# A float32 decoder trunk on one core: weights split in pairs of units, block sums over both depth halves, and one seven-product set computed plainly

## The chip, the cores and the metric

The kernel runs on one core of a Trainium2 chip. Times are device microseconds of that core. TensorE (PE in the profile) multiplies, VectorE (DVE) and ScalarE (ACT) do elementwise work, GpSimd (POOL) does small arithmetic and issues the DMAs that add into their destination, SyncE (SP) issues the other DMAs. Weights are read from memory once, as they are used.

## What is computed

A trunk of four layers on 256 rows of width 1024. Each layer is a half-step SwiGLU FFN, a token mixer with memory attention, and another half-step FFN, each between two normalizations. The kinds of mixer follow one another as A, B, C, A.

```python
def swiglu_ffn(x, w_gate_up, w_down):
    gate, up = jnp.split(x @ w_gate_up, 2, axis=-1)
    return (jax.nn.silu(gate) * up) @ w_down

for i in range(DEPTH):
    kind, j = i % 3, i // 3
    g = norm_g[i]
    x = x + 0.5 * rms_norm(swiglu_ffn(rms_norm(x, g[0]), ffn_w_gate_up[i, 0], ffn_w_down[i, 0]), g[1])
    h = rms_norm(x, g[2])
    mem_n = rms_norm(mem, mem_norm_g[i])
    ...
    x = x + rms_norm(y, g[3])
    x = x + 0.5 * rms_norm(swiglu_ffn(rms_norm(x, g[4]), ffn_w_gate_up[i, 1], ffn_w_down[i, 1]), g[5])
```

All of it is in float32. The hidden width of an FFN is 2816, that is 22 tiles of 128.

## The kernel before

**Three matmuls for one.** Every operand is split into a high part and a rest, `hi` and `lo`, of a type that PE multiplies in one pass. A product is then three matmuls: hi by hi, hi by lo, lo by hi. `split` (L311) makes both parts: ACT copies the source into `hi` (L312), and DVE subtracts `hi` from the source into `lo` (L313). Weights and activations go through it alike.

**The weight stream.** `plan()` lists all weight units in the order in which they are used. A unit has up to 1024 columns on 128 partitions, 512 KB. `load_next` (L244) fetches a raw unit into one of RAW = 5 buffers, on SP's queue. `split_next` (L291) takes the next unit of the plan, splits it into one `hi` and one `lo` tile of a ring of RING = 10, and fetches another raw unit. `take` hands a split unit to the code that multiplies; `slot(free)` is called after the matmuls of a unit, counts `free` units as released, and calls `pump`, which splits up to two units ahead while fewer than `released + RING - 1` have been split.

**An FFN** (`ffn`, L537) computes its hidden columns in six sets, `WIDTH = (4, 4, 2, 4, 4, 4)` tiles of 128. Set 0 runs while the second half of the rows is still being normalized: eight units, gate and up, are held for two passes (`first_set`). Sets 2 ("e") and 4 are plain: each unit is multiplied by both row halves, 12 matmuls of 512 columns a unit, and a set of four tiles has eight units. Sets 1, 3 and 5 are in `SEVEN`: gate and up for both row halves are a 2 x 2 block product, which `seven` (L635) makes with seven products instead of eight (Strassen's way, in Winograd's form). A product has two "S" units, one for each half of its depth (`h`), and each has six matmuls. The activations' block sums are made once an FFN (`sums`, L601).

**The weights' blocks.** For a seven-product set the four blocks b11, b12, b21, b22 of the weights are loaded raw into `quad` tiles (`load_quad`, L260), in eight loads of 512 KB, one a slot, in the order b11, b21, b12, b22. The operands of the seven products are b11, b21, b11 + (b12 + b22), b12 + b22, the third less b22, b21 plus the third, and b22. `operand` (L282) makes them half by half: when a half of b22 has been issued, a DMA of POOL's adds it into b12 (`gather`, L271); for operand 2 DVE adds b12 into b11 (L285) and another gather adds that into b21; for operand 4 DVE subtracts b22 from b11 (L288). An operand can be split only once all its loads have been issued (`can_split`, `quads_for`).

**The rest of an FFN.** In `seven`, products accumulate in three tiles of PSUM; intermediate sums are copied out by ACT (`snap`, L632) and combined by DVE (L644, L655, L661, L666, L667). `turned` transposes a finished set for the down projection and splits it into `hh` and `hl` (`eh` and `el` for set 2). `fill(n)` multiplies `n` units of the down projection ("D") between products; FILL says how many go where. The last eight D units are held for the two row halves; in the second pass the normalization of the first half (`ln_stages`, L361) and its transposes (L403) run beside it. The result of that is the next stage's `xt`.

**Mixers** take their weights from the same stream ("R", "C", "K", "V", "O" units). `snap` is a tag of four buffers, used for the copies above, for the squares of the normalization, for `xf` (the transposed activations that `sums` starts from) and for the memory's rows.

**The order on each engine** is made when the program is built: a planner goes through the instructions with its own estimates of their cost, and gives each engine the earliest instruction in program order that it holds ready. On the chip each engine then runs its list in that order, and what waits holds up what is behind it.

Of the kernel before, what the change touches and what calls it, by code (L numbers as in the profile page):

```python
# [10 lines left out]
F32 = mybir.dt.float32  # L11
F32R = mybir.dt.float32r
# [3 lines left out]
ALU = mybir.AluOpType  # L16
AX = mybir.AxisListType

P = 128
# [11 lines left out]
LN_EPS = 1e-5  # L31
BIG = 1e30
RING = 10
RAW = 5
HELD = 8
GRP = 4

# [18 lines left out]
WIDTH = (4, 4, 2, 4, 4, 4)  # L56
SETS = len(WIDTH)
FIRST = tuple(sum(WIDTH[:s]) for s in range(SETS))
SEVEN = (1, 3, 5)
FILL = {1: (2, 2), 2: (2,), 3: (2, 0), 4: (1, 1), 5: (2, 2)}  # L60
QUADS = 8


def ffn_chunks(l, f):
    order = []
    nd = 0

    def fill(n):
        nonlocal nd, order
        order += [("D", l, f, nd + i) for i in range(n)]  # L70
        nd += n

    for s in range(SETS):
        if s in SEVEN:
# [50 lines left out]
def load_order():  # L125
    order = []
    for key in plan():
        if key[0] != "S":
            order.append(key)
        elif key[4:] == (0, 0):  # L130
            order += quads(*key[1:4])
    return order


def unit_shape(key):
# [70 lines left out]
class Trunk:  # L206
    def __init__(self, ctx, tc, io):
        self.ctx, self.tc, self.nc, self.io = ctx, tc, tc.nc, io
        pool = lambda name, bufs=1, **kw: ctx.enter_context(tc.tile_pool(name=name, bufs=bufs, **kw))
        self.const = pool("const")  # L210
        self.wp = pool("wp")
        self.main = pool("main")
        self.small = pool("small", 4)
        self.ps = pool("ps", space=bass.MemoryType.PSUM)
        self.dram = pool("dram", space=bass.MemoryType.DRAM)
        self.plan = plan()
        self.offs = {}
# [5 lines left out]
        self.raw_order = [key for key in self.plan if key[0] != "S"]  # L223
        self.loaded = self.split_n = self.taken = self.released = 0
# [19 lines left out]
    def load_next(self):  # L244
        if self.loaded == len(self.raw_order):
            return
        key = self.raw_order[self.loaded]
        a, b = unit_shape(key)
        t = self.wp.tile([P, 1024], F32, tag="raw", name="raw", bufs=RAW)
        self.fetch(t[:, :a * b], key)  # L250
        self.raws.append((t, a * b))
        self.loaded += 1

    def new_quad(self, fp, l, f, s):
# [5 lines left out]
    def load_quad(self):  # L260
        key = self.quad_loads.popleft()
        q, h = key[4:]
        if h == 0:
            pool, tag = ((self.main, "mgh"), (self.quad_pool, "q22"), (self.main, "mgl"), (self.main, "rows"))[q]
            self.quad[q] = pool.tile([P, 2, 1024], F32, tag=tag, name="quad")
        self.fetch(self.quad[q][:, h, :], key)
        if q == 3:
            self.gather(self.quad[1][:, h, :], self.quad[3][:, h, :])

    def gather(self, x, y):  # L270
# [2 lines left out]
    def quads_for(self, key):  # L273
        if self.quad is None or self.quad_set != key[1:4]:
            return None
        return max(0, len(self.quad_loads) - (QUADS - ((2 * key[4] if key[4] < 2 else 6) + key[5] + 1)))

    def can_split(self):
        key = self.plan[self.split_n]
        return key[0] != "S" or self.quads_for(key) == 0  # L280

    def operand(self, op, h):  # L282
        b11, b12, b21, b22 = (t if t is None else t[:, h, :] for t in self.quad)
        if op == 2:
            self.nc.vector.tensor_tensor(out=b11, in0=b11, in1=b12, op=ALU.add)  # L285
            self.gather(b21, b11)
        elif op == 4:
            self.nc.vector.tensor_tensor(out=b11, in0=b11, in1=b22, op=ALU.subtract)  # L288
        return (b11, b21, b11, b12, b11, b21, b22)[op]

    def split_next(self):  # L291
        key = self.plan[self.split_n]
        hi = self.wp.tile([P, 1024], F32R, tag="hi", name="hi", bufs=RING)
        lo = self.wp.tile([P, 1024], F32R, tag="lo", name="lo", bufs=RING)
        if key[0] == "S":
            for _ in range(self.quads_for(key)):
                self.load_quad()
            self.split(hi, lo, self.operand(*key[4:]))
        else:
            t, n = self.raws.popleft()  # L300
            self.split(hi[:, :n], lo[:, :n], t[:, :n])
            self.load_next()
        self.ready.append((hi, lo))
        self.split_n += 1

    def pump(self, lag=1, most=2):
        while most and self.split_n < len(self.plan) and self.split_n < self.released + RING - lag and self.can_split():
            self.split_next()
            most -= 1

# [226 lines left out]
    def ffn(self, l, f, post_next, pre_next, last=False):  # L537
        nc, tc = self.nc, self.tc
        with tc.tile_pool(name=f"ffn{l}{f}", bufs=1, reuse_waits="tile") as fp:
# [15 lines left out]

            def turn_set(s, t):
                if t == 0:
                    if WIDTH[s] == 2:
                        hs[s] = tuple(fp.tile([P, 2, SEQ], F32R, tag=n, name=n) for n in ("eh", "el"))
                    else:  # L560
                        hs[s] = tuple(fp.tile([P, 4, SEQ], F32R, tag=n, name=n, bufs=2) for n in ("hh", "hl"))
                n = WIDTH[s]
                ps = self.rot()
                for k in range(n):
                    nc.tensor.transpose(ps[:, k * P:(k + 1) * P], T[s][t][:, k * P:(k + 1) * P], self.ident)  # L565
                self.split(*(h[:, :n, t * P:(t + 1) * P] for h in hs[s]),
                           ps[:, :n * P].rearrange("p (k t) -> p k t", k=n))
# [101 lines left out]
                product(s, 6, c, False, c12)  # L669
                fill(FILL[s][1])  # L670

            self.new_quad(fp, l, f, 1)
            first_set()
            left = sums()
            gn = {"pre": None}
# [102 lines left out]

    def mem_kv(self, l):
        nc = self.nc  # L780
        km = self.mp.tile([P, 2, SEQ], F32, name="km")
        vm = self.mp.tile([P, 2, SEQ], F32, name="vm")
        ps = self.rot().rearrange("p (a b) -> p a b", a=2)
        for c in range(2):
            self.cols_unit(ps[:, c, :], self.memg, self.take("K", l, c))
# [55 lines left out]
        return got[0]  # L841

    def q_mem(self, l, c0, xt):
        qm = self.mp.tile([P, 2, SEQ], F32, name="qm")
        ps = self.in_cols(l, c0, xt)
        self.nc.scalar.activation(out=qm, in_=ps, func=AF.Copy, scale=-0.125)
        return qm
# [500 lines left out]
```

## Time and profile before

| | us |
|---|---|
| median of 3 runs (lowest, highest) | 1889.15 (1886.43, 1889.77) |
| profiled execution | 1888.2 |
| its span, first to last instruction | 1886.4 |
| granted clock of TensorE, mean of the span | 0.996 |

| engine | busy, share of the span |
|---|---|
| TensorE, weight loads | 81% |
| VectorE | 81% |
| ScalarE | 60% |
| GpSimd | 8% |

Busy time of an engine is the time in which one of its instructions ran, by the profile. TensorE's matmuls overlap one another, so a busy TensorE need not be at its peak. A wait is the idle time of an engine just before an instruction, put down to what released it. The rows that carry the argument stand in the prediction.

### The profile page before, as it was taken

The page shows a single profiled execution, that of the slowest core. Times are in us where ns is not written, and L with a number is a line of the kernel's source. Part 1 is how long each engine was busy: PE and PEld are TensorE (multiplying, and loading weights), DVE is VectorE, ACT ScalarE, POOL GpSimd, SP SyncE. Part 2 cuts the span into 40 slices and gives each one's busy share as a digit, 9 for nine tenths or more (in the row PEclk, how much of TensorE's full clock was granted, in tenths as well). Part 3 has the DMA queues.
Part 4 walks back from the last instruction along what each step waited for, and adds up shares of the span by engine and source line. Part 5 has one row for each costly group of instructions (what it writes and reads, how often), then busy time and mean ns, then how long its engine had stood idle before and what let it go on. Part 6 is the DMA issues. An engine that isn't in the chain of part 4 may idle for free.

```text
span 1886.4 us, 25346 instructions
## 1 busy us (share of the span) xinstructions
PE 1842.0 (98%) x9310; PEld 1535.2 (81%) x9310; DVE 1537.1 (81%) x1868; ACT 1132.7 (60%) x1541; POOL 150.2 (8%) x211
## 2 busy tenths in 40 slices
PE   7999999999999999999999999999999999999998
PEld 5788887878788797778878889877788888987886
DVE  6888878987988768888789876879887988879884
ACT  5666656656665655656666666556665666656652
POOL 0000201000100100100010000010001000201000
PEclk9999999999999999999999999999999999999999
DMA  8886748776786662677668667358775786738862
GB/s 295 257 265 225 224 136 264 227 243 223 226 261 194 235 220 101 201 242 247 215 210 263 211 218 257 105 190 256 247 245 169 245 264 204 247 125 273 256 192 78
DMA packets 117692, 413.01 MB, mean 219 GB/s; under 512 B 13620, under 2 KB 18112, under 8 KB 117440
## 3 DMA queue, kind: packets, MB, share of 16 engines
q1 hardware_dynamic: 103568, 359.47, 54.2%
q0 software_dynamic: 14000, 51.92, 13.8%
q8 instruction: 73, 1.20, 0.3%
q14 instruction: 51, 0.42, 0.1%
HBM read 359.95 MB, written 1.06 MB: 191 GB/s over the span
## 4 chain that ended last, share of the span: by engine, by line
PE 41%; DVE 7%; DMA 3%; issue 2%; ACT 1%; POOL 1%; DVEq 0%; ACTq 0%; POOLq 0%
PE acc L696 12%; PE rot L624 9%; PE rot L337 5%; PE rot L339 5%; PE rot L338 5%; DVE lo L313 5%; PE acc L960 2%; DMA quad<-quad 2%; DMA quad<-in_w 1%; PE rot L565 1%; PE acc L880 1%; DVE quad L288 1%; PE rot L894 1%; PE rot L862 1%; ACT hi L312 0%
## 5 line engine op out<-in xcount | busy, mean ns | idle before, releaser
L313 DVE TENSOR_TENSOR lo<-raw,hi 128x1024 fp32r<-128x1024 f32 (+2 forms) x451 | 536.3, 1217 | 77.6 <-ACT hi L312 74.7
L312 ACT ACTIVATE hi<-raw 128x1024 fp32r<-128x1024 f32 (+2 forms) x451 | 463.2, 1051 | 198.3 <-DMA raw<-in_w 96.7
L312 ACT ACTIVATE hi<-quad 128x1024 fp32r<-128x1024 f32 x336 | 343.6, 1053 | 227.5 <-DVE quad L285 131.8
L313 DVE TENSOR_TENSOR lo<-quad,hi 128x1024 fp32r<-128x1024 f32 x336 | 397.5, 1219 | 20.7 <-ACT hi L312 19.9
L339 PE MATMUL rot<-hi,xtl 128*128 128x512 f32 (+3 forms) x816 | 312.8, 384 | 3.9 <-DVE xtl L313 3.9
L337 PE MATMUL rot<-hi,xth 128*128 128x512 f32 (+3 forms) x816 | 315.0, 386 | 0.4 <-ACT hi L312 0.4
L338 PE MATMUL rot<-lo,xth 128*128 128x512 f32 (+3 forms) x816 | 312.0, 382 | 0.3 <-DVE lo L313 0.3
L624 PE MATMUL rot<-hi,sums 128*128 128x512 f32 x768 | 255.1, 398 | 16.2 <-ACT snap L632 8.0
L696 PE MATMUL acc<-hi,hh 128*128 128x512 f32 x640 | 199.4, 391 | 0.0
L696 PE MATMUL acc<-lo,hh 128*128 128x512 f32 x640 | 198.9, 390 | 0.0
L696 PE MATMUL acc<-hi,hl 128*128 128x512 f32 x640 | 197.9, 390 | 0.0
L624 PEld LDWEIGHTS rot<-hi,sums 128*128 128x128 f32 x768 | 145.8, 190 | 52.9 <-ACT snap L632 12.3
L339 PEld LDWEIGHTS rot<-hi,xtl 128*128 128x128 f32 x816 | 153.7, 188 | 37.0 <-DVE xtl L313 8.3
L337 PEld LDWEIGHTS rot<-hi,xth 128*128 128x128 f32 x816 | 153.8, 189 | 29.2 <-ACT hi L312 1.0
L338 PEld LDWEIGHTS rot<-lo,xth 128*128 128x128 f32 x816 | 153.8, 188 | 29.2 <-DVE lo L313 0.5
L624 PE MATMUL rot<-lo,sums 128*128 128x512 f32 x384 | 151.2, 394 | 2.1 <-DVE lo L313 2.1
L271 POOL DMA_DIRECT2D quad<-quad x96 | 83.7, 897 | 837.6 <-DMA quad<-in_w 394.5
L696 PEld LDWEIGHTS acc<-hi,hl 128*128 128x128 f32 x640 | 119.6, 188 | 26.9 <-DVE hl L313 2.2
L696 PEld LDWEIGHTS acc<-lo,hh 128*128 128x128 f32 x640 | 119.9, 188 | 24.7
L696 PEld LDWEIGHTS acc<-hi,hh 128*128 128x128 f32 x640 | 119.7, 188 | 24.5
L624 PE MATMUL rot<-hi,xtl 128*128 128x512 f32 x288 | 112.1, 389 | 0.0
L624 PE MATMUL rot<-hi,xth 128*128 128x512 f32 x288 | 112.0, 389 | 0.0
(214 smaller groups left out, 2571.3 us busy)
## 6 DMA issues: line engine op xcount, KB each, us to landing
raw<-in_w SPq DMA_DIRECT2D x440, 512.0 KB, 4.8
quad<-in_w SPq DMA_DIRECT2D x192, 512.0 KB, 5.1
quad<-quad POOLq DMA_DIRECT2D x96, 512.0 KB, 4.7
gpre<-in_norm_g SPq DMA_DIRECT2D x8, 512.0 KB, 6.3
gpost<-in_norm_g SPq DMA_DIRECT2D x8, 512.0 KB, 3.4
memraw<-in_mem_t SPq DMA_DIRECT2D x32, 128.0 KB, 3.6
g<-in_norm_g SPq DMA_DIRECT2D x8, 512.0 KB, 6.7
raw<-in_w SPq DMA_DIRECT2D x8, 384.0 KB, 4.1
```

The costliest lines, as they stand in the source:

```text
L271: self.nc.gpsimd.dma_start(out=x, in_=y, accum_op=ALU.add)
L288: self.nc.vector.tensor_tensor(out=b11, in0=b11, in1=b22, op=ALU.subtract)
L312: self.nc.scalar.activation(out=hi, in_=src, func=AF.Copy)
L313: self.nc.vector.tensor_tensor(out=lo, in0=src, in1=hi.bitcast(F32), op=ALU.subtract)
L337: mm(out, a[0], b[0], start=start, stop=False)
L338: mm(out, a[0], b[1], start=False, stop=False)
L339: mm(out, a[1], b[0], start=False, stop=stop)
L565: nc.tensor.transpose(ps[:, k * P:(k + 1) * P], T[s][t][:, k * P:(k + 1) * P], self.ident)
L624: nc.tensor.matmul(ps, a[i], w[j][:, kk, :], start=fresh and h == kk == i == j == 0, stop=h == kk == i == 1, skip_group_check=True)
L696: mm(ys[t][:, n * 512:(n + 1) * 512], x, y[:, 0, n * 512:(n + 1) * 512], start=(j == 0 and x is a[0] and y is w[0]), stop=(j == NF - 1 and ...
L862: nc.tensor.transpose(ps[:, i * P:(i + 1) * P], blocks[b0 + i], self.ident)
L960: self.nc.tensor.matmul(o["y"][t][:, h * 512:(h + 1) * 512], x, y[:, 0, h * 512:(h + 1) * 512], start=(j == 0 and x is a[0] and y is w[0]) ...
```

## The change

- The ring holds pairs. `groups` joins neighbouring units of the plan that have the same kind and layer (for "S" units the two halves of one product). A pair is loaded by two DMAs into one raw tile of 2048 columns (RAW = 3 of them instead of 5 of 1024) and split by one ACT and one DVE instruction of 2048 columns, into one of five `hi` and five `lo` tiles. Where a pair's units are narrower than 1024, each is split by itself. `pump` counts units, and may split two groups a slot.
- Block sums go over both halves at once: one DVE instruction of 2048 columns for operands 2 and 4, and one gather of 1 MB into b21. All eight quads must have been issued ahead of operand 2.
- In set 1 b22 is added into b12 by DVE, not by a gather. Sets 3 and 5 keep the gathers, half by half.
- In the first FFN of layer 0 set 1 is plain: gate and up units, `fill(2)` after each.
- FILL of set 4 is (2, 0) instead of (1, 1), in all FFNs.
- Set 2 uses the two `hh` and `hl` buffers instead of its own `eh` and `el`; `km`, `vm` and `qm` of the mixers move from the mixer's pool to the `snap` tag.

```diff
-RAW = 5
+RAW = 3
...
-SEVEN = (1, 3, 5)
-FILL = {1: (2, 2), 2: (2,), 3: (2, 0), 4: (1, 1), 5: (2, 2)}
+FILL = {1: (2, 2), 2: (2,), 3: (2, 0), 4: (2, 0), 5: (2, 2)}
...
+def seven_sets(l, f):
+    return (1, 3, 5) if l or f else (3, 5)
...
+def groups(order):
+    out = []
+    for key in order:
+        last = out[-1] if out else []
+        if len(last) == 1 and last[0][:2] == key[:2] and (key[0] != "S" or last[0][:5] == key[:5]):
+            last.append(key)
+        else:
+            out.append([key])
+    return out
...
-        key = self.raw_order[self.loaded]
-        a, b = unit_shape(key)
-        t = self.wp.tile([P, 1024], F32, tag="raw", name="raw", bufs=RAW)
-        self.fetch(t[:, :a * b], key)
-        self.raws.append((t, a * b))
+        t = self.wp.tile([P, 2048], F32, tag="raw", name="raw", bufs=RAW)
+        for i, key in enumerate(self.raw_order[self.loaded]):
+            a, b = unit_shape(key)
+            self.fetch(t[:, 1024 * i:1024 * i + a * b], key)
+        self.raws.append(t)
...
-        if q == 3:
+        if q == 3 and key[3] > 1:
             self.gather(self.quad[1][:, h, :], self.quad[3][:, h, :])
...
-        return max(0, len(self.quad_loads) - (QUADS - ((2 * key[4] if key[4] < 2 else 6) + key[5] + 1)))
+        return max(0, len(self.quad_loads) - (QUADS - (2 * key[4] + key[5] + 1 if key[4] < 2 else 8)))
...
-    def operand(self, op, h):
-        b11, b12, b21, b22 = (t if t is None else t[:, h, :] for t in self.quad)
-        if op == 2:
-            self.nc.vector.tensor_tensor(out=b11, in0=b11, in1=b12, op=ALU.add)
+    def operand(self, op):
+        add = lambda x, y, f: self.nc.vector.tensor_tensor(out=x, in0=x, in1=y, op=f)
+        b11, b12, b21, b22 = self.quad
+        if op == 4:
+            add(b11, b22, ALU.subtract)
+        elif op == 2:
+            if self.quad_set[2] == 1:
+                add(b12, b22, ALU.add)
+            add(b11, b12, ALU.add)
             self.gather(b21, b11)
-        elif op == 4:
-            self.nc.vector.tensor_tensor(out=b11, in0=b11, in1=b22, op=ALU.subtract)
-        return (b11, b21, b11, b12, b11, b21, b22)[op]
+        return (b11, b21, b11, b12, b11, b21, b22)[op].rearrange("p a b -> p (a b)")
...
-        key = self.plan[self.split_n]
-        hi = self.wp.tile([P, 1024], F32R, tag="hi", name="hi", bufs=RING)
-        lo = self.wp.tile([P, 1024], F32R, tag="lo", name="lo", bufs=RING)
+        g = self.groups[self.split_n]
+        hi = self.wp.tile([P, 2048], F32R, tag="hi", name="hi", bufs=RING // 2)
+        lo = self.wp.tile([P, 2048], F32R, tag="lo", name="lo", bufs=RING // 2)
...
+            t = self.raws.popleft()
+            n = [a * b for a, b in map(unit_shape, g)]
+            if n == [1024, 1024]:
+                self.split(hi, lo, t)
+            else:
+                for i, w in enumerate(n):
+                    h = slice(1024 * i, 1024 * i + w)
+                    self.split(hi[:, h], lo[:, h], t[:, h])
...
-        while most and self.split_n < len(self.plan) and self.split_n < self.released + RING - lag and self.can_split():
+        while most and self.split_n < len(self.groups) and self.units < self.released + RING - lag and self.can_split():
...
-                    if WIDTH[s] == 2:
-                        hs[s] = tuple(fp.tile([P, 2, SEQ], F32R, tag=n, name=n) for n in ("eh", "el"))
-                    else:
-                        hs[s] = tuple(fp.tile([P, 4, SEQ], F32R, tag=n, name=n, bufs=2) for n in ("hh", "hl"))
+                    hs[s] = tuple(fp.tile([P, 4, SEQ], F32R, tag=n, name=n, bufs=2) for n in ("hh", "hl"))
...
-            self.new_quad(fp, l, f, 1)
+            SEVEN = seven_sets(l, f)
+            if 1 in SEVEN:
+                self.new_quad(fp, l, f, 1)
...
-        km = self.mp.tile([P, 2, SEQ], F32, name="km")
-        vm = self.mp.tile([P, 2, SEQ], F32, name="vm")
+        km = self.main.tile([P, 2, SEQ], F32, tag="snap", name="km", bufs=4)
+        vm = self.main.tile([P, 2, SEQ], F32, tag="snap", name="vm", bufs=4)
...
-        qm = self.mp.tile([P, 2, SEQ], F32, name="qm")
+        qm = self.main.tile([P, 2, SEQ], F32, tag="snap", name="qm", bufs=4)
```

More of the change, by code (lines that the diff above doesn't have):

```diff
@@ L73, in ffn_chunks @@
     for s in range(SETS):
-        if s in SEVEN:
+        if s in seven_sets(l, f):
             for ops, n in zip(((0, 1, 2), (3, 4, 5, 6)), FILL[s]):
@@ L222, in __init__ @@
             o += P * a * b
-        self.raw_order = [key for key in self.plan if key[0] != "S"]
-        self.loaded = self.split_n = self.taken = self.released = 0
+        self.groups = groups(self.plan)
+        self.raw_order = [g for g in self.groups if g[0][0] != "S"]
+        self.units = self.loaded = self.split_n = self.taken = self.released = 0
         self.raws = deque()
@@ L275, in quads_for @@
             return None
-        return max(0, len(self.quad_loads) - (QUADS - ((2 * key[4] if key[4] < 2 else 6) + key[5] + 1)))
+        return max(0, len(self.quad_loads) - (QUADS - (2 * key[4] + key[5] + 1 if key[4] < 2 else 8)))
     def can_split(self):
-        key = self.plan[self.split_n]
+        key = self.groups[self.split_n][-1]
         return key[0] != "S" or self.quads_for(key) == 0
-    def operand(self, op, h):
-        b11, b12, b21, b22 = (t if t is None else t[:, h, :] for t in self.quad)
-        if op == 2:
-            self.nc.vector.tensor_tensor(out=b11, in0=b11, in1=b12, op=ALU.add)
+    def operand(self, op):
[7 more added lines that the diff above has]
+            add(b11, b12, ALU.add)
@@ L286, in operand @@
             self.gather(b21, b11)
-        elif op == 4:
-            self.nc.vector.tensor_tensor(out=b11, in0=b11, in1=b22, op=ALU.subtract)
-        return (b11, b21, b11, b12, b11, b21, b22)[op]
+        return (b11, b21, b11, b12, b11, b21, b22)[op].rearrange("p a b -> p (a b)")
     def split_next(self):
-        key = self.plan[self.split_n]
-        hi = self.wp.tile([P, 1024], F32R, tag="hi", name="hi", bufs=RING)
-        lo = self.wp.tile([P, 1024], F32R, tag="lo", name="lo", bufs=RING)
@@ L295, in split_next @@
-        if key[0] == "S":
-            for _ in range(self.quads_for(key)):
+        g = self.groups[self.split_n]
+        hi = self.wp.tile([P, 2048], F32R, tag="hi", name="hi", bufs=RING // 2)
+        lo = self.wp.tile([P, 2048], F32R, tag="lo", name="lo", bufs=RING // 2)
+        if g[0][0] == "S":
+            for _ in range(self.quads_for(g[1])):
                 self.load_quad()
-            self.split(hi, lo, self.operand(*key[4:]))
+            self.split(hi, lo, self.operand(g[0][4]))
@@ L299, in split_next @@
         else:
-            t, n = self.raws.popleft()
-            self.split(hi[:, :n], lo[:, :n], t[:, :n])
+            t = self.raws.popleft()
[6 more added lines that the diff above has]
+                    self.split(hi[:, h], lo[:, h], t[:, h])
             self.load_next()
-        self.ready.append((hi, lo))
+        for i in range(len(g)):
+            self.ready.append((hi[:, 1024 * i:1024 * i + 1024], lo[:, 1024 * i:1024 * i + 1024]))
@@ L304, in split_next @@
         self.split_n += 1
+        self.units += len(g)
     def pump(self, lag=1, most=2):
-        while most and self.split_n < len(self.plan) and self.split_n < self.released + RING - lag and self.can_split():
+        while most and self.split_n < len(self.groups) and self.units < self.released + RING - lag and self.can_split():
             self.split_next()
```

## The prediction

> **What bounds the kernel now.** I read the busy times first, then who TensorE (PE) waits for, then the stretches around the longest waits.
>
> ```profile
> PE 1842.0 (98%) x9310; PEld 1535.2 (81%) x9310; DVE 1537.1 (81%) x1868; ACT 1132.7 (60%) x1541; POOL 150.2 (8%) x211
> 876.14 2.72 PE acc L696 x12
> ```
>
> PE is busy nearly throughout, and twelve 512-column matmuls in a row take 2.72 us (a piece of the chain that ended last): 0.227 us each. So the change can win only what PE idles, and each matmul that it adds costs 0.227 us. The waits of PE, of the whole span:
>
> ```profile
> PE rot L403 <- DVE rows L389: 11.6, 6, 8.3
> PE rot L624 <- ACT snap L632: 8.0, 10, 1.6
> PE rot L624 <- DVE snap L655: 4.7, 5, 2.6
> PE rot L339 <- DVE xtl L313: 3.9, 6, 1.2
> PE rot L624 <- ACT hi L312: 3.4, 1, 3.4
> PE rot L624 <- DVE lo L313: 2.1, 1, 2.1
> PE rot L565 <- DVE T L588: 1.5, 1, 1.5
> ```
>
> Columns are total, times, longest. Of the 11.6, 8.3 is the start. The 3.4 and the 2.1 are one place, set 1 of the first FFN. L632, L655 and L588 are evacuations inside the seven-product sets of the other FFNs: 8.0 + 4.7 + 1.5 = 14.2 us at 16 places. L403 and L339 after the start are the stage boundaries: 3.3 + 3.9 = 7.2 us at 11 places. The long waits cost more than themselves, since the clock falls (stretch; PE, PEld, DVE, ACT, POOL busy; granted clock; DMA):
>
> ```profile
> 46.00:60.00 14.00, 11.71 (x38) 9.18 (x39) 13.56 (x13) 9.31 (x11) 1.36 (x2) 0.76 0.80 208
> 382.00:392.00 10.00, 7.38 (x27) 5.68 (x26) 9.52 (x11) 5.09 (x6) 0.00 (x0) 0.83 0.97 345
> 386.54 0.80 PE L624 MATMUL rot<-hi,sums 128*128 128x512 f32 x1 [2.62 <-DVE snap L655]
> ```
>
> 14.00 x 0.24 = 3.4 us at 46 and 10.00 x 0.17 = 1.7 us at 386. The first FFN's stall is thus 3.4 + 2.1 + 3.4 = **8.9 us**, the later sets' 14.2 + 1.7 = **15.9 us**.
>
> The Trainium skill (TensorE: Matmul & The Clock Gate, What's actually happening) states that the clock halves after an idle window of about 3.4 us. The wait of 2.62 us above was enough here, so the trace differs; by the rule the later sets would hold 14.2 us, and the forecast would be 0.7 us later.
>
> **The change part by part.**
>
> *First FFN, set 1 plain.* Seven products of 12 matmuls are 84; the plain set has 2 x 4 units of 12, 96. **+12 x 0.227 = +2.7 us.** Its eight units are ordinary raw units, ready in the ring; the sum L285 and its gather, for which PE waited at 46, go. **-8.9 us.** DVE and ACT are late next only if raw units are late, and the DMA queues, which carried four megabytes of quads here, are emptier.
>
> *The start.*
>
> ```profile
> 8.10 1.06 ACT L312 ACTIVATE hi<-raw 128x1024 fp32r<-128x1024 f32 x1 [2.16 <-DMA raw<-in_w]
> 10.57 1.06 ACT L312 ACTIVATE hi<-raw 128x1024 fp32r<-128x1024 f32 x1 [0.53 <-DMA raw<-in_w]
> 9.19 1.23 DVE L313 TENSOR_TENSOR lo<-raw,hi 128x1024 fp32r<-128x1024 f32 x1 [0.96 <-ACT hi L312]
> 10.68 0.63 PE L338 MATMUL rot<-lo,xth 128*128 128x512 f32 x1
> ```
>
> Raw units land at 8.10 and 10.57, and x1, issued between them, in the same stretch: 1.23 us per half megabyte. The first split now waits for the second half of its pair, which takes x1's place: +1.23. It is twice as wide. From 512 to 1024 columns ACT goes from 620 to 1053 ns, DVE from 685 to 1219:
>
> ```profile
> L312 ACT ACTIVATE hi<-quad 128x1024 fp32r<-128x1024 f32 x336 | 343.6, 1053 | 227.5 <-DVE quad L285 131.8 <-DVE quad L288 34.0 <-PE rot L339 19.5
> L312 ACT ACTIVATE sums<-xf 128x512 fp32r<-128x512 f32 x32 | 19.2, 620 | 9.9 <-DVE xf L607 9.8
> L313 DVE TENSOR_TENSOR lo<-quad,hi 128x1024 fp32r<-128x1024 f32 x336 | 397.5, 1219 | 20.7 <-ACT hi L312 19.9
> L313 DVE TENSOR_TENSOR sums<-xf,sums 128x512 fp32r<-128x512 f32 x32 | 21.8, 685 | 0.1
> ```
>
> Two more steps of the same slope give 1.92 us (ACT) and 2.29 us (DVE) at 2048 columns, +0.87 and +1.07. The first lo matmul moves from 10.68 to about 13.9: **+3.1 us** (1 if ACT and DVE let other work through first; 5 if the fourth pair, whose raw buffer is the first pair's, is late as well).
>
> *One split instead of two.* In a row the saving is small, for the engines already overlap the fixed part:
>
> ```profile
> 380.12 5.76 DVE L313 TENSOR_TENSOR lo<-raw,hi 128x1024 fp32r<-128x1024 f32 x5
> 385.80 0.68 DVE L655 TENSOR_TENSOR snap<-rot,snap 128x512 f32<-128x512 f32 x1
> 1277.53 1.99 ACT L312 ACTIVATE hi<-quad 128x1024 fp32r<-128x1024 f32 x2
> 1279.42 0.58 ACT L632 ACTIVATE snap<-rot 128x512 f32<-128x512 f32 x1
> 1280.05 0.50 PE L624 MATMUL rot<-hi,sums 128*128 128x512 f32 x1 [1.56 <-ACT snap L632]
> ```
>
> Five subtractions take 5.76, so one more adds 1.135, two 2.27; one of 2048 in a row is about 2.29 - 0.08 = 2.20. 0.07 us a pair, and some 390 pairs: DVE -27 us, ACT (1.99 for two against 1.92) about as much. None of it is on PE's path except where PE waits, and these rows show what it waits for there: L655 stands behind five splits on DVE, L632 behind two on ACT. Both orders are the planner's. What is queued behind a split now waits for twice its width, but the queue empties a little sooner.
>
> *Set 1 of the other seven FFNs.* b12 + b22 goes from a gather by DMA to one DVE addition of 2048 columns: 7 x 2.29 = +16 us of DVE. What goes is DVE's wait for the gather:
>
> ```profile
> 1270.93 1.22 DVE L285 TENSOR_TENSOR quad<-quad 128x1024 f32<-128x1024 f32 x1 [2.06 <-DMA quad<-quad]
> 1273.41 1.23 DVE L285 TENSOR_TENSOR quad<-quad 128x1024 f32<-128x1024 f32 x1 [0.65 <-DMA quad<-quad]
> 1276.28 1.22 DVE L313 TENSOR_TENSOR lo<-quad,hi 128x1024 fp32r<-128x1024 f32 x1
> 1286.01 0.50 PE L624 MATMUL rot<-hi,sums 128*128 128x512 f32 x1 [1.12 <-ACT snap L632]
> 1273.00:1300.00 27.00, 24.32 (x110) 19.60 (x109) 26.59 (x28) 19.81 (x25) 1.56 (x2) 1.00 0.76 231
> 1266.42 1.83 POOL L271 DMA_DIRECT2D quad<-quad  x2 [11.29 <-DMA quad<-in_w]
> ```
>
> 2.71 us idle against 2.29 us of work, so DVE gains 0.4 us, 0.4 more on five pairs and 0.2 on the two block sums that stay: 1.0 us by op 4. The last quad has landed when the gathers issue, at 1266.4; DVE's two additions, split and subtraction (2.29 + 2.29 + 1.92 + 2.29 = 8.8) could end at 1275.2, and the old chain ended with the split at 1276.28, at 1277.5. The path is shorter by up to 2 us; the waits seen behind it are 1.56 and 1.12 us. But DVE then works 26.59 of 27.00 us, so what counts is its lead of 1.0.
>
> *Sets 3 and 5.* The first gather stays in halves, the sum waits for both, and op 2's first half can't start alone: up to +1.07 us. The second gather becomes one of 1 MB; op 4's subtraction must wait until it has read b11. The nearest rows:
>
> ```profile
> quad<-quad POOLq DMA_DIRECT2D x96, 512.0 KB, 4.7
> cb<-cd POOLq DMA_DIRECT2D x1, 1536.0 KB, 7.0
> ```
>
> Some 7 us, under op 2, two fills and op 3: 48 x 0.227 = 10.9 us of PE. Hidden; without that cover some 2 us a set.
>
> Over the later sets the term lies between -15.9 (all waits gone) and +16 (each of 16 places one half split later, 0.87 or 1.07). DVE's lead of 1.0 us at set 1, about 0.8 at set 3 (11 pairs x 0.07), and places of 0.8 us on average (14.2 / 16) say that a little under half goes: I take **-7 us**.
>
> *Boundaries and mixers.* The normalizing chain runs between splits:
>
> ```profile
> 937.80 1.06 ACT L312 ACTIVATE hi<-raw 128x1024 fp32r<-128x1024 f32 x1 [0.29 <-PE acc L696]
> 938.95 1.06 ACT L385 ACTIVATE junk<-x 128x1024 bf16<-128x1024 f32 x1
> 943.10 3.49 DVE L313 TENSOR_TENSOR lo<-raw,hi 128x1024 fp32r<-128x1024 f32 x3
> 957.13 1.06 PE L403 MATMUL rot<-ident,rows 128*128 128x128 f32 x8 [0.48 <-DVE rows L389]
> ```
>
> A split of 2048 that begins at 937.8 would end 0.8 later than L385 began. PE covers a part with the rest of the D units. Bounds: -7 (all of the 7.2 gone) and +11 (11 places x 1). The row is nearest to a quarter of the upper end: **+2.5 us**.
>
> *At nothing.* hh and hl for set 2: the D units that free each buffer stand one set earlier in PE's order. FILL (2, 0) of set 4: the moved D unit hides g's evacuation, and 24 matmuls of set 5 (5.4 us) hide u's. km, vm, qm in the snap ring: one buffer is left for the squares, which ACT runs in order; the xf copies after it come behind the last reader. If that cover goes, a copy of 0.62 us, as the one of 512 columns above, per mixer. Raw: six units in flight instead of five, but a SyncE issue waits for a whole pair, and the quads stand behind it.
>
> Sum: -8.9 + 2.7 + 3.1 - 7 + 2.5 = **-7.6 us**. The profiled execution took 1888.2 us (span 1886.4), 1 us under the median 1889.15; 1888.2 - 7.6 = 1880.6, on the median's scale **1881.5**.
>
> **The rivals.**
>
> *Coarse queues (slower).* The wide splits delay what stands behind them more than the lead helps. For it: all 16 evacuations and 11 boundaries already wait behind splits, and the planner orders by its own estimates. Against: the lead of 1.0 and 0.8 us. A place costs about 1 us; the first FFN's -3.1 and the measurement's 3.8 are used up at 7 places, and from there it decides. At half of the 27: 1888.2 - 3.1 + 13.5 = 1898.6, some **1899**.
>
> The Trainium skill (Perfetto Trace Analysis, Optimizing Scalar/DVE Operations) gives this rival as a rule: where these engines aren't saturated but cause bubbles on others, "breaking up instructions may allow work to be completed sooner"; the change does the reverse. DVE at 81% and bubbles behind splits fit it, though not the 27 us from 1273 on, in which DVE has no gap.
>
> *Backlog gone.* The lead suffices everywhere and the start costs 1: -8.9 + 2.7 + 1 - 15.9 + 0 = -21: **1868**. For it: waits of 0.8 us on average. Against: the wait at 386 is 2.6, behind five splits.
>
> *Nothing left.* The start takes 5, the addition on DVE only replaces the gather's wait, so that the sets keep all but 2 us of theirs, and the boundaries pay 3: -8.9 + 2.7 + 5 - 2 + 3 = -0.2: **1889**. That is also the case in which the pairs don't do what they should.
>
> **How the numbers follow.** Forecast 0.45 (1876 to 1885), backlog gone 0.15, nothing left 0.18, coarse queues 0.22 (1893 to 1906). 0.2% is 3.8 us, about what a measurement of this kernel can tell from no change. Faster 0.45 + 0.15 = 0.60, same 0.18, slower 0.22. The range runs from 1868, the middle of the fast rival, to 1897, short of the middle of the slow one: some 0.08 and 0.11 stay outside.
>
> **What would show it.** PE's waits for L312 and L313 at 46 us are gone, with no stretch of low clock before 60. The first matmul from lo comes at 13 to 14 us. Gathers: 7 + 16 x 3 = 55 instead of 96, 23 of them 1 MB. DVE's total falls by some 10 us (-27 + 16) and ACT's by more. PE's waits for L632, L655 and L588 sum to 7 to 9 us. It is wrong if these waits grow beyond 14.2, if L403 and L339 after the start exceed 11, if PE waits for raw units in the first FFN, or if softmax steps of the mixers, which I took as unmoved, appear among the waits.

## The result and the profile after

The changed kernel takes **1955.86 us** (median of 4 runs, 1954.34 to 1958.93); the kernel before took 1889.02 beside it. The ratio is 1.0358 (95% interval 1.034 to 1.0376): slower by about 67 us, where 1881.5 was forecast. Line numbers below are those of the changed kernel: L338 and L339 are the split, L655, L678 and L690 the evacuations and combinations in `seven`, L298 the sums of quads, L588 the transposes of a finished set (for the down projection), L429 those of a stage boundary, and L767 the last product of a plain set (SiLU of gate times up).

First the page, as before: busy time by engine, then the two groups of gathers (KB each, median us from issue to landing).

```profile
PE 1859.4 (95%) x9322; PEld 1538.9 (79%) x9322; DVE 1507.2 (77%) x1431; ACT 1071.1 (55%) x1149; POOL 112.0 (6%) x170
...
quad<-quad POOLq DMA_DIRECT2D x23, 1024.0 KB, 6.9
quad<-quad POOLq DMA_DIRECT2D x32, 512.0 KB, 8.9
```

The engines that feed PE have *less* to do than before (DVE by 30 us, ACT by 62), and PE waits more: its span less its busy time was 1886.4 - 1842.0 = 44.4 us and is 1953.8 - 1859.4 = 94.4. The other 17 us of the span are a longer busy time. The twelve added matmuls are 2.7 of it; the rest is put down here to no single cause. A stop costs a little more than its wait, though: the matmul that follows it takes 0.50 us in the rows below, where one in a row takes 0.39, and at 391.46 us, for one, the next begins 0.34 us later, where matmuls in a row come every 0.227.

The groups of instructions by shape (us in total, mean ns of one, then the idle time before them and what ended it) give the new prices:

```profile
L339 DVE TENSOR_TENSOR lo<-quad,hi 128x2048 fp32r<-128x2048 f32 x161 | 365.7, 2285 | 44.1 <-ACT hi L338 43.9
L338 ACT ACTIVATE hi<-quad 128x2048 fp32r<-128x2048 f32 x161 | 305.3, 1909 | 252.7 <-DVE quad L298 213.7 <-PE rot L365 8.9 <-PE acc L721 7.8
L298 DVE TENSOR_TENSOR quad<-quad 128x2048 f32<-128x2048 f32 x53 | 121.2, 2287 | 74.1 <-DMA quad<-quad 57.5 <-issue 13.1 <-DVE T L767 3.5
```

One split of 2048 columns costs 2.285 and 1.909 us, as estimated (2.29 and 1.92). What is new is the other column. ACT's wait for sums of quads was 131.8 + 34.0 = 166 us and is 213.7; DVE's wait for `hi` in splits of quads was 19.9 and is 43.9, with half as many splits: subtraction and copy of one pair now stand one after the other in full, where two halves overlapped.

PE's waits (us in total, times, longest), the largest:

```profile
PE rot L647 <- ACT snap L655: 20.9, 19, 2.0
PE rot L429 <- DVE rows L415: 15.7, 11, 8.3
PE rot L365 <- DVE xtl L339: 14.7, 13, 2.8
PE rot L588 <- DVE T L767: 9.7, 7, 2.2
PE rot L647 <- DVE snap L678: 5.9, 7, 1.4
PE rot L588 <- DVE T L690: 4.8, 1, 4.8
```

In the later sets PE waits 36.5 us at 33 places for L655, L678 and L767, where it waited 14.2 at 16 for L632, L655 and L588 of the kernel before. These are not quite the same lines. L632 and L655 of before are L655 and L678 now: 12.7 us then, 26.8 now. L588 of before (the product of set 0) is L611 now and fell from 1.5 to 0.3. L767 (the product of set 4) is new among the waits. The boundaries after the start (15.7 - 8.3 + 14.7) hold 22.1 where they held 7.2. One place is new, the 4.8 us for L690, and it lies in the first FFN. Here are three stretches by window, the two of the prediction and the one around the new wait (columns as in the prediction), and what ACT, DVE and PE ran at that wait, from the timeline:

```profile
46.00:60.00 14.00, 14.00 (x68) 11.68 (x67) 8.62 (x7) 6.69 (x7) 0.00 (x0) 1.00 0.87 317
100.00:150.00 50.00, 45.23 (x192) 37.08 (x191) 35.82 (x26) 23.43 (x18) 2.61 (x3) 0.93 0.72 236
382.00:392.00 10.00, 9.36 (x36) 7.31 (x35) 8.36 (x8) 6.71 (x6) 0.00 (x0) 0.87 0.67 247
```

```profile
120.61 0.68 DVE L689 TENSOR_TENSOR snap<-rot,snap 128x512 f32<-128x512 f32 x1
124.92 1.91 ACT L338 ACTIVATE hi<-raw 128x2048 fp32r<-128x2048 f32 x1 [6.54 <-DMA raw<-in_w]
126.86 2.29 DVE L339 TENSOR_TENSOR lo<-raw,hi 128x2048 fp32r<-128x2048 f32 x1 [5.56 <-ACT hi L338]
129.07 0.68 DVE L690 TENSOR_TENSOR T<-T,snap 128x512 f32<-128x512 f32 x1
129.81 1.54 PE L588 MATMUL rot<-ident,T 128*128 128x128 f32 x6 [4.77 <-DVE T L690]
```

The stall at 46 is gone: PE is busy for all of the 14 us, at full clock. At 382 the clock has fallen as it had before (0.87, and 0.83 then), but not at the same work: PE had waited 2.00 us for L655 ahead of a set's third product here, and for the combination ahead of the seventh there. Another stall has come at 125. L690, which PE needs, stands on DVE behind a subtraction that waits for its copy, which waits for a raw pair to land, 6.54 us on ACT. L690 reads neither the pair nor its split. The last thing that it needed, L689, had ended at 121.29, and it stood in the queue for 7.8 us more; it is the place in the queue that costs.

A seven-product set of layer 2's first FFN shows the same on both queues, again from the timeline:

```profile
1058.89 2.29 DVE L298 TENSOR_TENSOR quad<-quad 128x2048 f32<-128x2048 f32 x1
...
1061.27 1.92 ACT L338 ACTIVATE hi<-quad 128x2048 fp32r<-128x2048 f32 x1 [4.39 <-DVE quad L298]
...
1063.61 1.90 ACT L338 ACTIVATE hi<-quad 128x2048 fp32r<-128x2048 f32 x1
...
1065.41 0.57 ACT L655 ACTIVATE snap<-rot 128x512 f32<-128x512 f32 x1
...
1066.04 0.50 PE L647 MATMUL rot<-hi,sums 128*128 128x512 f32 x1 [1.16 <-ACT snap L655]
...
1070.44 4.48 DVE L339 TENSOR_TENSOR lo<-raw,hi 128x2048 fp32r<-128x2048 f32 x2
...
1074.84 0.68 DVE L678 TENSOR_TENSOR snap<-rot,snap 128x512 f32<-128x512 f32 x1
...
1075.58 0.50 PE L647 MATMUL rot<-hi,sums 128*128 128x512 f32 x1 [0.83 <-DVE snap L678]
```

ACT stands idle 4.39 us until the whole sum of 2048 columns is done, then runs its splits, and L655 comes after them; DVE runs two wide subtractions, 4.48 us, ahead of L678. PE stops for both.

### The profile page after: what moved, and what is told of

Same layout as the page of the kernel before. It is cut to its first block, busy times and chain, and to the rows that moved or that the text cites. A ratio compares the mean times of both kernels' runs of the same rounds, so it can differ in the third digit from the quotient of the medians.

```text
span 1953.8 us, 23890 instructions
## 1 busy us (share of the span) xinstructions
PE 1859.4 (95%) x9322; PEld 1538.9 (79%) x9322; DVE 1507.2 (77%) x1431; ACT 1071.1 (55%) x1149; POOL 112.0 (6%) x170
## 5 line engine op out<-in xcount | busy, mean ns | idle before, releaser
L339 DVE TENSOR_TENSOR lo<-raw,hi 128x2048 fp32r<-128x2048 f32 (+2 forms) x235 | 520.0, 2223 | 128.2 <-ACT hi L338 126.0
L338 ACT ACTIVATE hi<-raw 128x2048 fp32r<-128x2048 f32 (+2 forms) x235 | 435.6, 1861 | 243.7 <-DMA raw<-in_w 126.5
L338 ACT ACTIVATE hi<-quad 128x2048 fp32r<-128x2048 f32 x161 | 305.3, 1909 | 252.7 <-DVE quad L298 213.7
L339 DVE TENSOR_TENSOR lo<-quad,hi 128x2048 fp32r<-128x2048 f32 x161 | 365.7, 2285 | 44.1 <-ACT hi L338 43.9
L365 PE MATMUL rot<-hi,xtl 128*128 128x512 f32 (+3 forms) x848 | 325.1, 386 | 14.7 <-DVE xtl L339 14.7
L363 PE MATMUL rot<-hi,xth 128*128 128x512 f32 (+3 forms) x848 | 328.7, 388 | 3.5 <-ACT xth L338 1.6
L364 PE MATMUL rot<-lo,xth 128*128 128x512 f32 (+3 forms) x848 | 325.8, 384 | 1.0 <-DVE lo L339 1.0
L721 PE MATMUL acc<-hi,hh 128*128 128x512 f32 x704 | 221.1, 391 | 0.0
L721 PE MATMUL acc<-hi,hl 128*128 128x512 f32 x704 | 217.0, 389 | 1.2 <-DVE hl L339 1.2
L721 PE MATMUL acc<-lo,hh 128*128 128x512 f32 x704 | 218.0, 390 | 0.0
L298 DVE TENSOR_TENSOR quad<-quad 128x2048 f32<-128x2048 f32 x53 | 121.2, 2287 | 74.1 <-DMA quad<-quad 57.5
```

Of the source, the lines that this page charges most:

```text
L298: add = lambda x, y, f: self.nc.vector.tensor_tensor(out=x, in0=x, in1=y, op=f)
L338: self.nc.scalar.activation(out=hi, in_=src, func=AF.Copy)
L339: self.nc.vector.tensor_tensor(out=lo, in0=src, in1=hi.bitcast(F32), op=ALU.subtract)
L363: mm(out, a[0], b[0], start=start, stop=False)
L364: mm(out, a[0], b[1], start=False, stop=False)
L365: mm(out, a[1], b[0], start=False, stop=stop)
```

## The experiments

All ratios are against the kernel before, run on the same chip, with 95% intervals. The first theory was the *coarse queues* of the prediction: the width of the split delays what stands behind it. Its rivals were the whole sums of quads, and the small edits that had been costed at nothing.

### One part of the change alone

**b_plain** adds the plain set 1 of the first FFN to the kernel before:

```diff
+def seven_sets(l, f):
+    return (1, 3, 5) if l or f else (3, 5)
...
```

> The kernel before with set 1 plain in the first FFN, nothing else. By the forecast's own terms: +2.7 us for 12 matmuls, -8.9 us for the waits at 46 us, the start unchanged: about 1883 us. If the first FFN's loss in the changed kernel comes from the plain set itself (its raw units late), this run is slower than before, 1890 to 1897.

1884.13 us, ratio 0.9985 (0.9975 to 0.9995). This is the fastest kernel found, but it brings 0.15% (0.05 to 0.25%, some 3 us) where stall less matmuls made 6.2. Two windows of it:

```profile
46.00:60.00 14.00, 14.00 (x63) 11.59 (x62) 8.62 (x10) 6.87 (x10) 0.00 (x0) 1.00 0.90 319
60.00:100.00 40.00, 37.82 (x166) 30.89 (x165) 27.06 (x30) 18.75 (x24) 3.66 (x4) 0.96 0.70 209
```

The stall is gone, and behind it PE loses 2.2 us in waits and 40 x 0.04 = 1.6 us in clock, where the kernel before lost neither. Its waits show the step that was late next, DVE's part of `hl`:

```profile
PE acc L701 <- DVE hl L316: 2.2, 1, 2.2
```

**b_fill** and **b_mem** each make one edit that was costed at nothing: FILL of set 4, and the moves of `eh`, `el`, `km`, `vm`, `qm`.

```diff
-FILL = {1: (2, 2), 2: (2,), 3: (2, 0), 4: (1, 1), 5: (2, 2)}
+FILL = {1: (2, 2), 2: (2,), 3: (2, 0), 4: (2, 0), 5: (2, 2)}
```

```diff
-        km = self.mp.tile([P, 2, SEQ], F32, name="km")
+        km = self.main.tile([P, 2, SEQ], F32, tag="snap", name="km", bufs=4)
...
```

> The kernel before with FILL of set 4 at (2, 0), nothing else. If the wait of the transposes for T of set 4 (9.7 us at 7 places in the changed kernel) comes from the missing D unit after the up units, this run is 5 to 10 us slower than before and shows that wait. If it comes from wide splits ahead of that multiplication on VectorE, it stays within 2 us of before.

> The kernel before with hh and hl for set 2 and with km, vm and qm in the snap ring, nothing else. If the forecast's zero for these was right, within 2 us of before. If the snap ring is what slows the mixers (16 us over four of them in the changed kernel), 10 to 16 us slower.

0.9998 (0.9986 to 1.0009) and 0.9999 (0.9988 to 1.0011): in the kernel before, both are nothing, as costed.

**b_sums** takes only the whole sums of quads and the 1 MB gathers, with set 1's b12 + b22 on DVE, into the kernel before; **b_whole** the same but leaves set 1 to gathers; **b_set1** only the addition on DVE, in halves.

```diff
+        if op == 4 and h == 0:
+            add(b11, b22, ALU.subtract)
+        elif op == 2 and h == 0:
+            if self.quad_set[2] == 1:
+                add(b12, b22, ALU.add)
+            add(b11, b12, ALU.add)
+            self.gather(b21, b11)
...
```

> The kernel before with the block sums over both halves (one instruction of 2048 columns, one 1 MB gather, set 1's b12 sum on VectorE), but splits and ring in single units. If the sums' granularity is what slows the FFNs, 15 to 35 us slower than before. If it is the paired ring and its splits, within 5 us of before.

> The kernel before with block sums of 2048 columns and one gather of 1 MB into b21, all eight loads ahead of operand 2, but set 1's b12 sum still by gathers. If the width of the sums is what cost 38 us with the whole part, 1915 to 1930 us; if set 1 on VectorE did it, within 5 us of before.

> The kernel before with only this: in set 1 VectorE adds b22 into b12, in halves of 1024 columns, instead of a gather. The forecast's term (VectorE gains 0.4 us of lead a set) says 0 to -5 us. If VectorE's 16 us of added work comes onto the path, +5 to +16 us.

1924.6 us, ratio 1.0202 (1.0187 to 1.0217); 1.0258 (1.0233 to 1.0282); 1.0001 (0.9988 to 1.0015). Whole sums alone cost 2% in a kernel with narrow splits, and the addition on DVE takes half a per cent of that back; alone it is neutral, as the term said (a lead of 0.4 us a set). The waits of b_sums sit mostly where one expects them, at the evacuations behind the sums (its L635 is L632 of the kernel before, L658 is L655), which held 12.7 us and hold 29.4. The transposes of the boundaries (L406) hold 10.1 us after the start, where they held 3.3:

```profile
PE rot L406 <- DVE rows L392: 17.9, 8, 7.8
PE rot L627 <- DVE snap L658: 17.7, 16, 1.7
PE rot L627 <- ACT snap L635: 11.7, 19, 1.5
```

### One part of the change undone

**a_halves** splits every pair of the changed kernel by two ACT and two DVE instructions of 1024 columns. **a_sums** keeps the wide splits and makes sums and gathers in halves (set 1's b12 + b22 by gather again). **a_narrow** does both, and sums and splits each half ahead of the next.

```diff
-                self.split(hi, lo, t)
+                for i, w in enumerate(n):
+                    h = slice(1024 * i, 1024 * i + w)
+                    self.split(hi[:, h], lo[:, h], t[:, h])
...
```

```diff
+        for h in range(2):
+            if op == 4:
+                add(b11[:, h], b22[:, h], ALU.subtract)
+            elif op == 2:
+                add(b11[:, h], b12[:, h], ALU.add)
+                self.gather(b21[:, h], b11[:, h])
...
```

> The changed kernel with every pair split by two ACT and two VectorE instructions of 1024 columns; ring, loads and block sums as changed. Theory A (wide instructions hold up what is queued behind them): most of the loss comes back, 1905 to 1925 us. Theory B (pairs in the ring and in the raw buffers make the weights late): little comes back, 1945 to 1960 us.

> The changed kernel with its block sums and gathers in halves again (set 1 by a gather too), splits still 2048 wide. If the sums over both halves cost in the changed kernel what they cost alone (38 us), about 1918 us. If the wide splits are the cost and the sums only lengthen the same waits, 1940 to 1956 us.

> The changed kernel with splits of 1024 columns and block sums and gathers in halves, each half summed and split before the next: what is left of the change are the pairs of the ring and of the raw buffers, FILL, the memory moves and the plain set. If pairing the buffers costs nothing by itself (theory A whole: instruction width is all), 1883 to 1890 us. If the 21 us left with narrow splits belong to the pairs, 1900 to 1908 us.

| kernel | splits | sums | us | ratio (interval) |
|---|---|---|---|---|
| the change | wide | whole | 1955.86 | 1.0358 (1.034 to 1.0376) |
| a_sums | wide | halves | 1955.72 | 1.0365 (1.0336 to 1.0393) |
| a_halves | narrow | whole | 1908.24 | 1.0107 (1.0092 to 1.0122) |
| a_narrow | narrow | halves | 1902.61 | 1.0076 (1.0048 to 1.0105) |

The width of the splits is worth some 50 us (1955.86 - 1908.24 = 47.6, and 53.1 between the other two); the sums, beside wide splits, nothing. Beside narrow splits in pairs the sums cost 5.6 us (1908.24 - 1902.61), far less than the 38 us that they cost alone in b_sums; why, no run shows. PE's waits in a_narrow, where L651 is the copy by ACT, L663 the first sum in `seven`, L607 the product of set 0, and L425 and L361 are the boundaries:

```profile
PE rot L425 <- DVE rows L411: 11.9, 8, 7.9
PE rot L361 <- DVE xtl L335: 10.7, 13, 2.7
PE acc L717 <- DVE hl L335: 3.9, 5, 2.5
PE rot L643 <- ACT snap L651: 3.6, 7, 1.2
PE rot L584 <- DVE T L607: 2.1, 3, 1.1
PE rot L915 <- DVE pt L888: 1.9, 2, 1.7
PE rot L643 <- DVE snap L663: 1.6, 1, 1.6
```

The three lines that held 14.2 us before the change (L632, L655 and L588; here L651, L674 and L607) hold 5.7 (3.6 + 2.1, and nothing for L674). L663 takes 1.6 and a wait of the D units for `hl` (L717) 3.9, both new; the boundaries keep 14.7 (11.9 - 7.9 + 10.7). The same set of layer 2 as above runs there without a stop:

```profile
1029.85 0.60 ACT L651 ACTIVATE snap<-rot 128x512 f32<-128x512 f32 x1
1030.33 2.02 ACT L334 ACTIVATE hi<-quad 128x1024 fp32r<-128x1024 f32 x2
...
1037.78 2.36 DVE L335 TENSOR_TENSOR lo<-raw,hi 128x1024 fp32r<-128x1024 f32 x2 [0.80 <-ACT hi L334]
...
1040.06 0.68 DVE L674 TENSOR_TENSOR snap<-rot,snap 128x512 f32<-128x512 f32 x1
```

ACT's copy L651 now stands ahead of the splits, and the DVE instruction that was L678 behind 2.36 us of subtractions, not 4.48. How much of this is the width and how much the order that the planner makes of the narrower pieces, the runs don't show.

**a_act** and **a_dve** keep the width on one engine only. The edit shown is that of a_act; in a_dve the two lists of slices change places.

```diff
+        for h in (slice(0, 2048),):
+            self.nc.scalar.activation(out=hi[:, h], in_=src[:, h], func=AF.Copy)
+        for h in (slice(0, 1024), slice(1024, 2048)):
+            self.nc.vector.tensor_tensor(out=lo[:, h], in0=src[:, h], in1=hi.bitcast(F32)[:, h], op=ALU.subtract)
...
```

> The changed kernel with ACT's part of a split in one instruction of 2048 columns and VectorE's in two of 1024. If what counts is that TensorE's evacuations stand behind a wide instruction of ACT, it stays near the changed kernel: 1940 to 1956 us. If VectorE's width counts, near the kernel with both in halves (1908 us): 1905 to 1920 us.

> The changed kernel with ACT's part in two instructions of 1024 columns and VectorE's in one of 2048. The mirror of the last: 1905 to 1920 us if ACT's width counts, 1940 to 1956 us if VectorE's does. If either alone brings half, both runs lie at 1925 to 1940 us.

1985.25 us, ratio 1.0514 (1.0489 to 1.0538), and 1951.3, ratio 1.0339 (1.0317 to 1.0361). Either width alone costs about as much as both; ACT's alone costs more. One of the two was expected near the kernel with narrow splits, or both halfway; neither came. DVE's waits for `hi` in splits of quads, 19.3 us in a_halves and 43.9 in the change, are 35.3 in a_act and 46.3 in a_dve. In a_act DVE's half-width subtractions must wait for the whole copy all the same, and PE waits for L773, the product at the end of a plain set:

```profile
PE rot L594 <- DVE T L773: 26.5, 5, 6.8
```

Why this exceeds the change itself, with the same ACT instructions and finer DVE ones, isn't settled.

**a_fill** sets FILL of set 4 back to (1, 1) in the changed kernel; **a_seven** sets the first FFN's set 1 back to seven products (the diffs above, reversed).

> The changed kernel with FILL of set 4 back at (1, 1); its two D units are then groups of one. If the missing D unit makes the transposes wait for T of set 4, about 8 to 10 us faster than the changed kernel (1946 us). If that wait is due to wide splits, or single groups cost as much as they win, within 3 us of it.

> The changed kernel with seven products in set 1 of the first FFN too. By the forecast's terms 12 matmuls go (-2.7 us) and a wait of some 9 us comes: 1962 us. If the plain set is what costs the first FFN its 8 us, it is faster than the changed kernel, about 1948 us.

1936.68 us, ratio 1.0262 (1.0245 to 1.028): an edit that is worth nothing in the kernel before costs 1% (19 us) beside wide splits, twice the 8 to 10 us expected. Part of the 19 can be another thing: with (1, 1) the two D units of an FFN are no longer neighbours, so they are no pair and are split one by one, and no run parts this from their place. PE's 9.7 us for T of L767 and the 4.8 for L690 don't appear in the waits of a_fill, and its waits for L655 are 4 us less:

```profile
PE rot L647 <- ACT snap L655: 16.8, 15, 2.2
```

a_seven: 1955.43 us, ratio 1.036 (1.0341 to 1.0379), no difference, where 1962 or 1948 was expected: what the plain set wins at 46 it loses at 125.

### The pairs in the ring

a_narrow has narrow splits and half sums and is still slower than before. To place the rest, the spans are cut where, at each stage boundary, the last transpose of the first half of the rows begins. Between such cuts the eight FFNs of the changed kernel are 47.8 us longer than before and the four mixers 19.6; those of a_narrow are 1.3 us *shorter* and 16.7 longer. Each figure comes from one execution: in b_plain and b_set1, which leave the mixers as they were, the same cuts make the mixers 3.7 and 2.2 us longer. The windows of mixer C, in three kernels: before, after, a_narrow:

```profile
1125.63:1246.00 120.37, 120.37 (x872) 103.64 (x871) 89.15 (x213) 68.91 (x147) 5.51 (x10) 1.00 0.51 170
```

```profile
1161.00:1289.18 128.18, 122.70 (x873) 104.73 (x871) 87.16 (x197) 66.87 (x129) 5.93 (x10) 0.99 0.45 162
```

```profile
1124.32:1251.08 126.76, 122.28 (x873) 104.11 (x872) 89.21 (x212) 68.19 (x146) 4.36 (x10) 0.99 0.44 158
```

Before, PE never stops in this stage; in the other two it stops for 5.5 and 4.5 us. In a_narrow the waits there include 1.7 us for `pt` and 1.5 for `p`, softmax steps: the sign that the prediction named for itself.

**a_raw1** gives a_narrow six single raw buffers; **a_ring** further goes back to five, to `eh` and `el`, and to the mixers' own `km`, `vm`, `qm`, so that only the pairs in the ring, FILL and the plain set are left of the change.

```diff
-RAW = 3
+RAW = 6
...
-        self.raw_order = [g for g in self.groups if g[0][0] != "S"]
+        self.raw_order = [key for key in self.plan if key[0] != "S"]
...
```

> The kernel with narrow splits and sums but pairs in the ring (1902.6 us), with raw buffers of one unit, six of them, each refilled when its own half is split. If the mixers' 17 us come from raw units that are loaded and freed in pairs, 1885 to 1892 us; if from the hi and lo tiles that are taken and freed in pairs, 1898 to 1905 us.

> As a_raw1, but with five raw buffers and with km, vm, qm and set 2's eh and el where they were before: only the hi and lo tiles are in pairs, beside FILL and the plain set. If the paired hi and lo tiles alone slow the mixers, the mixers still take 12 to 18 us more than before and the run 1895 to 1905 us. If it is the snap ring together with pairs, the mixers are as before and the run takes 1883 to 1890 us.

1904.39 us, ratio 1.0091 (1.0072 to 1.0109), and 1916.16, ratio 1.0149 (1.0121 to 1.0177). The mixers stay 15.9 and 17.2 us longer than before: raw buffers and the snap tag are not the cause there. But a_ring takes more than the 1895 to 1905 us expected, 11.8 us more than a_raw1. By the same cuts that lies in the FFNs: 13.2 us longer than before in a_ring, 0.6 in a_raw1. So beside pairs the sixth raw buffer or the memory moves, or both, save some 12 us, although the moves are worth nothing in the kernel before; no run parts the two.

**b_burst** keeps a ring tile for each unit but splits the two units of a pair in one slot (so up to four units a slot, where it was two); **b_tile** gives a pair one ring tile but splits unit by unit.

```diff
-            self.split_next()
+            for _ in range(self.pos[self.split_n][1]):
+                self.split_next()
...
```

```diff
+        i = self.pos[self.split_n][0]
+        if i == 0:
+            self.pair = (self.wp.tile([P, 2048], F32R, tag="hi", name="hi", bufs=RING // 2),
+                         self.wp.tile([P, 2048], F32R, tag="lo", name="lo", bufs=RING // 2))
...
```

> The kernel before, still with ten ring tiles of one unit each, but the pump splits the units of a pair one after the other in one slot, as in the changed kernel, instead of one unit a slot. Theory A (bursts): in the mixers the two splits of a burst stand together in front of the softmax steps in the queues of ACT and DVE; the mixers grow by 10 us or more, the FFNs by 0 to 13 as with pairs in the ring alone, so 1897 to 1915. Theory B (shared tiles): a burst costs nothing while each unit has a tile of its own; 1884 to 1890.

> The kernel before with five ring tiles of a pair each, but split unit by unit, one a slot, as before. Theory A (bursts): sharing a tile costs nothing, since both units of the pair that held the tile are released when the next one is split; 1884 to 1890. Theory B (shared tiles): a split waits for the matmuls of both units of the pair that held its tile, not of one, and the mixers grow by 10 us or more; 1897 to 1915. If both kernels cost about half, both hold.

1908.13 us, ratio 1.0107 (1.0088 to 1.0127), and 1918.52, ratio 1.0167 (1.0144 to 1.0189), the second a little above what was expected. Both cost. By the same cuts the mixers are 6.0 and 9.7 us longer, together 15.7, about the 16 to 17 of the pairs; that the two add up in this way is not shown, and 6.0 is not far above the 3.7 of b_plain. The FFNs, too, are longer in both, by some 11 and 19, which the rest of the change must offset in a_narrow. The 12 us between a_ring and a_raw1 can be a part of that; what the rest is, no run shows. That a shared tile is held until both of its units have been multiplied is the reason that fits b_tile; it was not seen directly.

## Why the prediction was wrong

**What held.** The prices of the wide instructions; 55 gathers, 23 of 1 MB; busy time falling on DVE and ACT; the stall at 46 us gone. The start, too: its first matmul from `lo`, forecast for about 13.9, comes at 13.74, behind a split of the forecast size:

```profile
13.74 0.80 PE L364 MATMUL rot<-lo,xth 128*128 128x512 f32 x1 [1.05 <-DVE lo L339]
```

**The step that failed** is *One split instead of two*, with the -7 us taken over the later sets. It saw, and quoted, that L655 stood behind five splits and L632 behind two, and then weighed against this a lead of 1.0 and 0.8 us that the engines would gain by their smaller sums. The lead is a saving over eleven or more pairs in a row; the delay falls on whatever is queued behind the one split that runs when PE needs it, or, worse, behind a split that waits. The sums fell as forecast (more, on DVE: 30 us, not 10), and it didn't matter: the waits of these sets went from 14.2 to 36.5 us, 26.8 of them at the two evacuations that had held 12.7. The sign "wrong if these waits grow beyond 14.2" came true. Undoing the width alone gives back 47.6 us of 67 (a_halves), and with the sums in halves too (a_narrow) the three lines of the forecast hold 5.7, less than the 7 to 9 that it had for the change. How much of this is the width itself, and how much the order that the planner makes of wide pieces, stays open.

**The slower rival was the right one, and too small.** *Coarse queues* priced 27 places, the ones at which PE already waited, at 1 us, and expected half of them. But a delay makes new places: 33 in the later sets, where 16 were, at 36.5 / 33 = 1.1 us each. The list of present waits shows where slack is already used up; it doesn't show the places that have only a little of it, and here these were about as many. The rule of the Trainium skill that the prediction set beside this rival (Perfetto Trace Analysis, Optimizing Scalar/DVE Operations: break instructions up where the engines aren't saturated but cause bubbles on others) is borne out: DVE was at 81% and is at 77%, and a_halves is faster by 47.6 us than the change.

**The whole sums**, which the forecast counted as a gain of 0.2 to 1.0 us a set, cost 2.0% alone (b_sums). Under wide splits they cost nothing more (a_sums). That a wide split must wait for both halves of its sum anyhow would explain it, but no run shows that. The clause "op 2's first half can't start alone: up to +1.07 us" was the right thing to look at, but it was only an end of the range.

**Boundaries and mixers** had +2.5 us, at most +11. The boundaries' waits grew by 14.9 us (7.2 to 22.1), over the bound of 11 that the prediction gave as a sign against itself. In the mixers the 19.6 us are mostly not the width but the pairs: 16.7 of them stay in a_narrow. No term stood for that; The "softmax steps of the mixers, which I took as unmoved" named the place, and put no price on it.

**At nothing.** The memory moves are nothing alone (b_mem); beside pairs they, or the sixth raw buffer, save some 12 us (a_raw1 against a_ring). FILL (2, 0) is nothing alone and, with the pair that it makes of two D units, costs 19 us here: its cover, "24 matmuls of set 5 (5.4 us)" over T's product, is enough in the old queue and isn't beside wide splits, where that product is what PE waits for (9.7 us at 7 places). Both were costed beside the old queue.

**First FFN.** -8.9 + 2.7 was borne out in its parts (the stall gone, twelve matmuls more), but not in its sum: alone it gives some 3 us, for the next late step takes 2.2 and the clock 1.6 (b_plain), and in the changed kernel nothing. What would be late next was answered with raw units or nothing; it was DVE's `hl`, and beside wide splits L690 behind a raw pair.

## What to carry to other kernels

Where engines run in order and PE waits for short steps behind long ones, price a wider instruction by what it delays, at every place where such a step follows it, not only at those that already wait, and not by the fixed cost it saves: here 0.07 us a pair, some 27 us of DVE's time by the forecast's estimate, stood against some 50 us of run time lost. Two instructions of which the second reads what the first writes overlap only as far as they are cut into pieces, so merging either of them makes the second wait longer (35.3 and 46.3 us against 19.3). Cost "free" edits beside the new queue, and treat the sharing of a buffer by two units, and the issue of two units in one slot, as changes of their own.

## What the hardware showed that was not expected

- From 1024 to 2048 columns a subtraction on DVE goes from 1219 to 2285 ns and a copy on ACT from 1053 to 1909 ns: merging two in a row saves almost nothing, as they overlap by some 0.09 us anyway (4.48 us for two of 2.285).
- A gather of 1 MB takes 6.9 us from issue to landing (median of 23), less than the 8.9 that one of 512 KB takes beside it in the same kernel, and than twice the 4.7 of before; what else was on the queues at the time is not known here.
- TensorE's clock fell after waits of 2.62 us (before) and 4.77 us (after): the granted clock of 50 us around the latter is 0.93, that is 3.5 us lost on top of a wait of 4.8. It fell after one of 2.00 us too (after, 0.87 from 382 to 392), but not after one of 2.81 us (after, which ended at 211.81; 1.00 from 205 to 220). So the length of the wait alone doesn't say whether it falls.
